# Mixing stage of a two-layer hybrid decoder: probability products in fp32, queries normed inside the scores, the key factor as a logarithm, Silu on ScalarE, and other constants for the order

## Chip, cores and metric

The kernel runs on one core of a Trainium2 chip. The metric is the device time of one execution in microseconds (us); the time of the kernel before is the median of its runs. The engines are PE (TensorE; PEld is its weight load), DVE (VectorE), ACT (ScalarE), POOL (GpSimd) and SP, which here issues all DMAs.

## What is computed

Two layers over 256 rows of 1024 numbers, all in fp32. Each layer is a SwiGLU half step, a mixing step with two groups of heads side by side, and a second SwiGLU half step. Cut to what the change touches:

```python
for l in range(2):
    x = x + 0.5 * swiglu(rmsnorm(x), ...)           # D_FF = 2816
    proj = rmsnorm(x) @ w_in[l]                      # q, k/v of three branches, gates, hq, hf, hi, hg
    # attention: 8 query heads of 64 in 2 groups; three branches of keys
    q = norm_rope(q); k_cmp, k_sel, k_win = norm_rope(...)   # RMS norm per head, then rotation
    o = g0 * softmax(q @ compressed_k) @ compressed_v + g1 * softmax(q @ k_sel) @ v_sel + g2 * softmax(q @ k_win) @ v_win
    # recurrence: 4 heads of 128, chunks of 64 rows
    q = silu(hq); f = lb + (1 - lb) * sigmoid(hf); k = 1 - f; v = hi
    b = cumsum(log f)
    a[t, s] = sum_k q[t, k] * exp(b[t, k] - b[s, k]) * k[s, k]    # s <= t, else 0
    o = rmsnorm(a @ v + carried state) * silu(hg)
    x = x + concat(attention, recurrence) @ w_out[l]
    x = x + 0.5 * swiglu(rmsnorm(x), ...)
```

## The kernel before

Rows are in two halves of 128 (`h` = 0, 1). All matrix products with weights run as three fp32r products, hi times hi, hi times lo and lo times hi: each number is split into an fp32r part `hi` (a copy on ACT) and a rest `lo` (a subtraction on DVE, at times on POOL). Weights arrive by DMA in units of 512 KB, and each unit is split the same way while the unit before it is used, so the stream itself costs one ACT copy (line 334) and one DVE subtraction (line 347) of 128x1024 for each unit.

The program is written out by a planner at build time (`Sched.run`). Every piece of work is a generator that hands in one operation at a time with a planned cost and the engines that may take it. The planner always issues the operation with the earliest planned start plus a penalty; the penalties stand in `PEN`, `STEP`, `PREP`, `FLOW`, `BIAS`, and `LAG` and `OUT_ORDER` shape the weight stream. So the constants set nothing but the order of instructions on each engine and which engine takes an operation that has a choice. Most operations are issued by helpers, so they share a line: 347 is a DVE `tensor_tensor`, 350 one on POOL, 334 an `activation`, 343 a DVE copy, 358 a DVE `tensor_scalar`, 360 one on POOL, 376 the power for inverse square roots on POOL, 382 transposes. They are told apart by their tiles.

In a mixing step the in-projection streams through in the order q, kv, kw, hf, hq, hi, hg. Meanwhile:

- `q_task` squares the projected queries (ACT), sums (DVE, line 896), takes the inverse root (POOL), multiplies (DVE, `buf<-acc,qst`) and frees the accumulator, then rotates. `kv_task`, `kw_task` and `values` split the values into `vh` and `vl`.
- `log_task` and `level_task` build the recurrence. `level_task` walks over seven block sizes; at each it makes left factors, exp of the running sum `S` times the key factor `kk` (`hx<-hx,kk`), and right factors, exp of `P` times the query (`hx<-hx,xn`), for small products on PE (line 1368) that are put into `ad` (line 1374).
- `head_task` (16 in each mixing step) makes scores on PE (lines 1174 and 1175), adds the mask and takes the row maximum in one DVE instruction for each of two branches (line 1178), scales the maxima by -1/8 (`mx<-mx`, line 358 or 360), takes Exp on ACT, and multiplies by gate over sum.
- `turn_task` (12 in each mixing step) transposes four heads' probabilities, copies them to `pth` (ACT), subtracts to get `ptl` (DVE); `attend_task` then issues for each of two halves three fp32r products of 256 columns with `vh` and `vl` (lines 1144 to 1146). `cmp_task` handles the compressed branch; its product (line 1158) is in plain fp32.
- `hq_task` and `hg_task` take Sigmoid on ACT and multiply by the projection on DVE (`xn<-hx,acc` and `G<-G,acc`).

Then the out-projection runs: the attention part needs `att`, the recurrence part needs `ho` of `out_task`.

Of the kernel before, what the change touches and what calls it, by code (L numbers as in the profile page):

```python
# [23 lines left out]
SCALE = DH ** -0.5  # L24
# [25 lines left out]
FIRST = (-0.3, -0.4, 0.5, 1.3, 0.1, 0.6, 0.9, 0.2)  # L50
LAG = 4
NBUF = 14
OUT_ORDER = ((0, 0), (0, 1), (1, 0), (1, 1))
# [3 lines left out]
PEN = {"norm_turn": 0.1, "next_gain": 2.25, "gates_task": 0.15, "compress_task": -0.05, "level_task": 0.25,  # L57
       "boot": -1.0, "first_gain": -0.3, "first_norm": -0.25, "pad": 3.35, "hi_task": -3.8, "load_stream": 3.25,
       "done": 0.25, "kv_task": 0.65, "turn": 2.65, "load_w1": 3.15, "mix_prepare": -0.2, "c_turn": -3.3,
       "f_task": 0.25, "q_turn": 0.05, "kw_task": -6.1, "q_task": 0.6, "hg_task": 0.75, "hq_task": 0.45,  # L60
       "last_product": -0.15, "k_turn": 0.15, "products": 0.05, "turn_task": -0.1, "attend_task": -0.05,
       "out_task": 0.05, "k_task": 0.4, "cmp_task": -0.1, "first_turn": -0.65, "head_task": -0.1, "log_task": 0.15}
STEP = {'h': -0.16, 'g': 0.03, 'r': 0.0}
PREP = (-0.2, 0.25, 0.55, 0.75)
FLOW = (0.25, 0.15, 0.15)
BIAS = {'POOL': 0.1, 'ACT': -0.05}
# [56 lines left out]
class Sched:  # L123
# [85 lines left out]
    def emit(self, t, eng, start, end, fn):  # L209
        fn()  # L210

    def run(self):
        while self.tasks:
# [28 lines left out]
            self.emit(t, eng, end - cost, end, fn)  # L242
# [42 lines left out]
def rel(x, *objs):  # L285
    return ("rel", x, objs)
# [18 lines left out]
class Trunk(Sched):  # L305
# [251 lines left out]
    def start(self):  # L557
# [14 lines left out]
        self.padded = [per.tile([128, 4, 320], F32R, name=n) for n in ("vh", "vl")]  # L572
# [10 lines left out]
    def pad(self):  # L583

        nc = self.nc
        vh, vl, gv, vcb = self.padded
        for t in [gv, vcb] + self.pcs:
            yield self.G(0.25, lambda: nc.gpsimd.memset(t, 0.0))
        z = vcb[:, 0:1, 0, :64].to_broadcast([128, 4, 64])
        for v in (vh, vl):  # L590
            for o in (0, 128, 256):
                yield self.G(0.97, lambda: nc.gpsimd.tensor_copy(v[:, :, o:o + 64], z))
        yield put("padded")
# [267 lines left out]
    def mix(self, l):  # L861
# [24 lines left out]
        def q_task(h, ps):  # L886
            yield wait(("open", p))
            yield wait(("prepared", l))
            bufs = yield acq("buf", 3)
            (pair,) = yield acq("pth")  # L890
            sq, xr, t2 = [x.rearrange("p (n d) -> p n d", d=64) for x in bufs]
            qd = [x.rearrange("p (n a d) -> p n a d", n=4, a=2) for x in pair]
            src = ps.rearrange("p (n d) -> p n d", d=64)
            st = M["qst", h]
            yield A(sq, src, AF.Square)
            yield V(512, lambda: nc.vector.tensor_reduce(st[:, 0], sq, AX.X, OP.add))
            yield from self.rope_norm(st, (H, DH))
            x_ = yield tt(xr, src, st[:, 0, :, None].to_broadcast([128, H, 64]), OP.mult)
            yield rel(f"acc{h}", ps)
            cg = self.cg[:, h, 0:1].to_broadcast([128, H, 64])  # L900
            a_ = [(yield tt(sq, xr, cg, OP.mult, pool=True))]
            for o, i in swap:
                a_.append((yield tt(t2[:, :, o], xr[:, :, i], self.sg[:, h, 0:1, o].to_broadcast([128, H, 32]), OP.mult,
                                    pool=True, after=[x_])))
            for b, d in enumerate(qd):
                c = slice(4 * b, 4 * b + 4)
                hi = d[:, :, 0]
                yield tt(sq[:, c], sq[:, c], t2[:, c], OP.add, pool=True, after=a_)
                yield self.copy(hi, sq[:, c])
                yield tt(d[:, :, 1], sq[:, c], hi.bitcast(F32), OP.subtract, pool=True)  # L910
                yield put(key("qd", h, b))
                sub(q_turn(h, b, pair, d), deps=self.keys[key("qd", h, b)])
            yield rel("buf", *bufs)
# [17 lines left out]
        def values(h, br, src):  # L931

            c = lambda v: v[:, 2 * br + h, 64:].rearrange("p (g d) -> p g d", g=2)[:, :, :64]
            yield from self.split(c(M["vh"]), c(M["vl"]), src)
# [169 lines left out]
        def attend_task(h, g):  # L1104
            for x in (("k", h), ("k", 0), ("q", h, g), ("g", h)):
                yield wait(key(*x))
# [23 lines left out]
            vh, vl, vcb = M["vh"], M["vl"], M["vcb"]  # L1130
# [4 lines left out]
            for i, (so, vi) in enumerate(tiles):  # L1135
                yield wait(key("pt", h, g, i))
                yield wait(key("v", vi % 2, vi // 2))
                th, tl = M["pt", h, g, i]

                def pv(e):  # L1140
                    o = 64 + 128 * g - 64 * e
                    c = slice(256 * e, 256 * e + 256)
                    f = nc.tensor.matmul
                    f(po[:, :256], vh[:, vi, o:o + 128], th[:, c], start=(i == 0 and e == 0), stop=False)
                    f(po[:, :256], vl[:, vi, o:o + 128], th[:, c], start=False, stop=False)
                    f(po[:, :256], vh[:, vi, o:o + 128], tl[:, c], start=False, stop=False)  # L1146

                for e in range(2):
                    yield P(0.36, lambda: pv(e))
                yield rel("pth", (th, tl))  # L1150
# [15 lines left out]
        def head_task(h, g, r, part, pr, mx):  # L1166

            qs, kh, kl, gt = M["qs", h], M["kh"], M["kl"], M["gt", h]
            mxr, smr = mx[:, 0, r], mx[:, 1, r]
            a, b, segs = part  # L1170
# [6 lines left out]
            for br, o, n, mask in segs:  # L1177
                yield V(n, lambda: nc.vector.tensor_tensor_reduce(pr[r][:, o:o + n], ps[:, o:o + n], mask, 1.0, -BIG, OP.add, OP.max,  # L1178
                                                                  mxr[:, br:br + 1]))
            yield rel("short", ps)  # L1180
            yield ts(mxr, mxr, -SCALE, pool=True)
            for br, o, n, mask in segs:
                x = pr[r][:, o:o + n]
                yield A(x, x, AF.Exp, bias=mxr[:, br:br + 1], scale=SCALE, accum_out=smr[:, br:br + 1])
# [9 lines left out]
        def turn_task(h, g, i, so, pr):  # L1194
            (pt,) = yield acq("short")
            yield self.transposes([(pt[:, 128 * k:128 * k + 128], pr[r][:, so:so + 128]) for k, r in enumerate((0, 2, 1, 3))])
            ((th, tl),) = yield acq("pth")
            yield from self.split(th, tl, pt)
            M["pt", h, g, i] = th, tl
# [3 lines left out]
        def cmp_task(h, g):  # L1203
# [19 lines left out]
            yield V(64, lambda: nc.vector.tensor_reduce(m, x, AX.X, OP.max))  # L1223
            yield tt(x, x, m[:, :, None].to_broadcast([128, R, 16]), OP.subtract, pool=True)
            yield A(x, x, AF.Exp, scale=SCALE)
# [35 lines left out]
        def log_task(h):  # L1261
# [12 lines left out]
            d_ = yield G(0.46, lambda: nc.gpsimd.memset(s_, 0.0))  # L1274
# [3 lines left out]
        def hq_task(c, ps):  # L1278
            yield wait(("open", p))
            (e,) = yield acq("hx")  # L1280
            yield A(e, ps, AF.Sigmoid)
            v = lambda x: x.rearrange("p (k h t) -> p k h t", k=2, h=2)
            yield tt(M["QQ"][:, :, 2 * c:2 * c + 2].rearrange("p h k t -> p k h t"), v(e), v(ps), OP.mult)
            yield rel(f"acc{c}", ps)
            yield put(key("hq", c))
            yield rel("hx", e)
# [7 lines left out]
        def hg_task(h, ps):  # L1294
            yield wait(("open", p))
            x = M["G2", h]
            yield A(x, ps, AF.Sigmoid)
            yield tt(x, x, ps, OP.mult)
# [8 lines left out]
        def level_task(h):  # L1307
# [9 lines left out]
            for i, hh in enumerate(LEVELS[1:] + [64]):  # L1317
# [11 lines left out]
                else:  # L1329
                    a_ = yield A(xl, sl, AF.Exp, after=prev + got)  # L1330
                    c_ = yield tt(xl, xl, kl, OP.mult, pool=True)
# [12 lines left out]
            yield tt(xc, xc, kk if h == 0 else q, OP.mult)  # L1344
# [115 lines left out]
        def opened(pool, p):  # L1460
# [3 lines left out]
            self.slots["hx"] = [(T([128, 512], f"hx{i}"), []) for i in range(4)]  # L1464
            self.slots["pth"] = [((T([128, 512], f"pth{i}", F32R), T([128, 512], f"ptl{i}", F32R)), []) for i in range(2)]
# [21 lines left out]
            M["vh"], M["vl"], M["gv"], M["vcb"] = self.padded  # L1487
# [64 lines left out]
```

## Time and profile before

| | |
|---|---|
| median of 3 runs (lowest to highest) | 1134.69 us (1132.74 to 1187.89) |
| profiled execution, its own time | 1132.6 us |
| its span, first to last instruction | 1130.8 us |
| busy: PE, DVE, ACT, POOL | 1090.8, 699.6, 577.1, 96.6 us |
| mean granted clock of PE | 0.972 of 2.4 GHz |

A group of instructions in the profile is one line, engine, operation and pair of tiles: `out<-in`, partitions x elements, count, then busy time in all, mean ns of one, and the idle time of the engine just before them. Tiles go by the names of the program (`short`, `acc` and `po` are PSUM; `kk`, `P`, `S`, `xn`, `mx`, `buf` are SBUF). Seen by stages, the two mixing steps lie at 205 to 394 us and 762 to 950 us; the rest are SwiGLU steps.

### The profile page before, as it was taken

The page shows a single profiled execution, that of the slowest core. Times are in us where ns is not written, and L with a number is a line of the kernel's source. Part 1 is how long each engine was busy: PE and PEld are TensorE (multiplying, and loading weights), DVE is VectorE, ACT ScalarE, POOL GpSimd, SP SyncE. Part 2 cuts the span into 40 slices and gives each one's busy share as a digit, 9 for nine tenths or more (in the row PEclk, how much of TensorE's full clock was granted, in tenths as well). Part 3 has the DMA queues.
Part 4 walks back from the last instruction along what each step waited for, and adds up shares of the span by engine and source line. Part 5 has one row for each costly group of instructions (what it writes and reads, how often), then busy time and mean ns, then how long its engine had stood idle before and what let it go on. Part 6 is the DMA issues. An engine that isn't in the chain of part 4 may idle for free.

```text
span 1130.8 us, 18755 instructions
## 1 busy us (share of the span) xinstructions
PE 1090.8 (96%) x7420; PEld 975.9 (86%) x7420; DVE 699.6 (62%) x1242; ACT 577.1 (51%) x911; POOL 96.6 (9%) x124
## 2 busy tenths in 40 slices
PE   6999999999889999999999999999997899999998
PEld 4999988898668799998889999888975788999986
DVE  5665544689985755554465555448898857555543
ACT  6544444467664554443454444435866645444432
POOL 3100000041121100000010000001403201000000
PEclk9999999999879999999999999999998699999999
DMA  7666666565501476666666666556544125666553
GB/s 223 209 197 172 189 185 188 161 174 168 169 20 38 149 207 185 186 185 187 188 179 195 187 179 187 185 168 187 165 137 131 38 75 168 196 180 186 185 160 120
DMA packets 154168, 186.16 MB, mean 165 GB/s; under 512 B 7568, under 2 KB 117984, under 8 KB 154080
## 3 DMA queue, kind: packets, MB, share of 16 engines
q1 hardware_dynamic: 154080, 184.96, 55.1%
q8 instruction: 58, 0.95, 0.3%
q14 instruction: 30, 0.25, 0.1%
HBM read 183.89 MB, written 1.05 MB: 164 GB/s over the span
## 4 chain that ended last, share of the span: by engine, by line
PE 85%; DVE 9%; DMA 2%; issue 2%; ACT 1%; POOL 1%; SPq 0%; DVEq 0%; ACTq 0%; POOLq 0%
PE acc L515 15%; PE acc L516 15%; PE acc L517 15%; PE acc L485 11%; PE acc L487 11%; PE acc L486 11%; PE short L382 2%; DVE lo L347 2%; DVE buf L1178 1%; PE short L1368 1%; DVE xn L690 1%; DMA lg<-in_hgrn_lb_logits_dram 1%; DVE hx L347 1%; PE po L1146 1%; DVE buf L358 1%
## 5 line engine op out<-in xcount | busy, mean ns | idle before, releaser
L347 DVE TENSOR_TENSOR lo<-raw,hi 128x1024 fp32r<-128x1024 f32 (+2 forms) x329 | 394.9, 1202 | 287.2 <-ACT hi L334 286.0
L334 ACT ACTIVATE hi<-raw 128x1024 fp32r<-128x1024 f32 (+2 forms) x337 | 351.6, 1045 | 317.4 <-PE acc L487 108.0
L515 PE MATMUL acc<-xh,hi 128*128 128x256 f32 x1408 | 399.2, 284 | 0.0
L517 PE MATMUL acc<-xh,lo 128*128 128x256 f32 x1408 | 398.4, 283 | 0.0
L516 PE MATMUL acc<-xl,hi 128*128 128x256 f32 x1408 | 398.4, 283 | 0.0
L515 PEld LDWEIGHTS acc<-xh,hi 128*128 128x128 f32 x1408 | 270.2, 192 | 0.2
L516 PEld LDWEIGHTS acc<-xl,hi 128*128 128x128 f32 x1408 | 270.3, 192 | 0.1
L517 PEld LDWEIGHTS acc<-xh,lo 128*128 128x128 f32 x1408 | 270.2, 192 | 0.0
L485 PE MATMUL acc<-hi,th 128*128 128x512 f32 x352 | 139.7, 397 | 0.0
L486 PE MATMUL acc<-lo,th 128*128 128x512 f32 x352 | 139.2, 395 | 0.0
L487 PE MATMUL acc<-hi,tl 128*128 128x512 f32 x352 | 139.2, 395 | 0.0
L485 PE MATMUL acc<-hi,xh 128*128 128x512 f32 (+1 forms) x240 | 95.8, 399 | 0.0
L487 PE MATMUL acc<-hi,xl 128*128 128x512 f32 (+1 forms) x240 | 91.7, 382 | 0.0
L486 PE MATMUL acc<-lo,xh 128*128 128x512 f32 (+1 forms) x240 | 91.2, 380 | 0.0
L487 PEld LDWEIGHTS acc<-hi,tl 128*128 128x128 f32 x352 | 66.1, 188 | 16.1
L486 PEld LDWEIGHTS acc<-lo,th 128*128 128x128 f32 x352 | 66.2, 188 | 15.5
L485 PEld LDWEIGHTS acc<-hi,th 128*128 128x128 f32 x352 | 66.2, 188 | 15.5
L334 ACT ACTIVATE sg<-acc 128x512 f32<-128x512 f32 (+1 forms) x46 | 26.2, 570 | 72.0 <-PE acc L517 68.8
L376 POOL TENSOR_TENSOR rs<-rs,half 128x1 f32<-128x1 f32 x12 | 7.0, 587 | 572.6 <-DVE rs L683 572.6
L487 PEld LDWEIGHTS acc<-hi,xl 128*128 128x128 f32 x240 | 45.4, 189 | 9.1 <-DVE xl L347 0.4
L485 PEld LDWEIGHTS acc<-hi,xh 128*128 128x128 f32 x240 | 45.5, 190 | 7.8
L486 PEld LDWEIGHTS acc<-lo,xh 128*128 128x128 f32 x240 | 45.5, 190 | 6.9
(230 smaller groups left out, 1100.1 us busy)
## 6 DMA issues: line engine op xcount, KB each, us to landing
raw<-in_ffn_w_down_dram SPq DMA_DIRECT2D x88, 512.0 KB, 4.2
raw<-in_ffn_w_gate_dram SPq DMA_DIRECT2D x80, 512.0 KB, 3.8
raw<-in_ffn_w_up_dram SPq DMA_DIRECT2D x80, 512.0 KB, 3.9
raw<-in_w_in_dram SPq DMA_DIRECT2D x48, 512.0 KB, 3.8
raw<-in_w_out_dram SPq DMA_DIRECT2D x16, 512.0 KB, 3.7
buf<-in_cmp_w_dram SPq DMA_DIRECT2D x16, 256.0 KB, 7.3
raw<-in_ffn_w_gate_dram SPq DMA_DIRECT2D x13, 256.0 KB, 2.8
raw<-in_ffn_w_up_dram SPq DMA_DIRECT2D x13, 256.0 KB, 3.1
```

The source lines that it names most:

```text
L334: return ("ACT", c, lambda: self.nc.scalar.activation(out, in_, func, **k), TABLES.get(func), False)
L347: alts = [("DVE", 0.065 + 0.00104 * n, lambda: self.nc.vector.tensor_tensor(out, a, b, op), None, not in_psum(a) and not in_psum(b))]
L358: lambda: self.nc.vector.tensor_scalar(out, a, s1, s2, **k), None, not in_psum(a))]
L382: self.nc.tensor.transpose(o, i, self.ident[:i.shape[0], :i.shape[0]])
L485: f(ps[:, :k.n], ah, hi[:, t, :k.n], start=st, stop=False)
L486: f(ps[:, :k.n], ah, lo[:, t, :k.n], start=False, stop=False)
L487: f(ps[:, :k.n], al, hi[:, t, :k.n], start=False, stop=sp)
L515: f(ps[:, c], hi[:, t, j], xh, start=u.first and c == t == 0, stop=False)
L516: f(ps[:, c], hi[:, t, j], xl, start=False, stop=False)
L517: f(ps[:, c], lo[:, t, j], xh, start=False, stop=u.last and c == 1 and t == 3)
L690: toks.append((yield self.V(576, lambda: nc.vector.scalar_tensor_tensor(self.XN[h][:, c], self.X[h][:, c], rs[:, 0:1], self.gains[0][:, c] ...
L1146: f(po[:, :256], vh[:, vi, o:o + 128], tl[:, c], start=False, stop=False)
```

## The change

Six edits of the mixing step and a new set of planner constants.

1. The transposed probabilities and the values are no longer split: `turn_task` makes one copy `th` (on ACT or DVE), `values` one copy `vh`, and each half is one fp32 product in place of three fp32r ones.
2. Queries are rotated straight out of PSUM without the norm. The norm factor, times -1/8, is a number per row and head (`nq`); the instruction of line 1178 multiplies by it and takes the minimum, so the scaling of the maxima is gone. `cmp_task` multiplies by it in an operation of its own. `attend_task` waits for it as well.
3. `log_task` puts log of the key factor into `S` where it wrote zeros, so that exp of `S` holds the key factor and six multiplications in each `level_task` go, and one more for `h` = 0.
4. `hq_task` and `hg_task` use Silu on ACT in place of Sigmoid and a product.
5. `pad` clears one tile of values with memsets where it cleared two with copies.
6. All the planner's constants are new, and the recurrence part of the out-projection takes its two column halves in the other order.

```diff
-LAG = 4
+LAG = 5
-OUT_ORDER = ((0, 0), (0, 1), (1, 0), (1, 1))
+OUT_ORDER = ((0, 0), (0, 1), (1, 1), (1, 0))
...
-       "done": 0.25, "kv_task": 0.65, "turn": 2.65, "load_w1": 3.15, "mix_prepare": -0.2, "c_turn": -3.3,
...
+       0.38, "kv_task": 0.73, "turn": 0.9, "load_w1": 2.81, "mix_prepare": 0.27, "c_turn": -3.2, "f_task": 0.07,
...
-BIAS = {'POOL': 0.1, 'ACT': -0.05}
+BIAS = {'POOL': 0.07, 'ACT': -0.49}
...
         def q_task(h, ps):
-            yield A(sq, src, AF.Square)
-            yield V(512, lambda: nc.vector.tensor_reduce(st[:, 0], sq, AX.X, OP.add))
-            yield from self.rope_norm(st, (H, DH))
-            x_ = yield tt(xr, src, st[:, 0, :, None].to_broadcast([128, H, 64]), OP.mult)
+            x_ = yield A(xr, src, AF.Square)
+            sub(q_norm(h, bufs[1], st), deps=[x_])
+            cg = self.cg[:, h, 0:1].to_broadcast([128, H, 64])
+            a_ = [(yield tt(sq, src, cg, OP.mult))]
+            for o, i in swap:
+                a_.append((yield tt(t2[:, :, o], src[:, :, i], self.sg[:, h, 0:1, o].to_broadcast([128, H, 32]), OP.mult)))
+            yield ("deps", a_)
             yield rel(f"acc{h}", ps)
...
+        def q_norm(h, buf, st):
+
+            yield V(512, lambda: nc.vector.tensor_reduce(st[:, 0], buf.rearrange("p (n d) -> p n d", d=64), AX.X, OP.add))
+            yield rel("buf", buf)
+            yield from self.rope_norm(st, (H, DH))
+            yield ts(st[:, 0], st[:, 0], -SCALE)
+            yield put(key("nq", h))
...
         def values(h, br, src):
-            yield from self.split(c(M["vh"]), c(M["vl"]), src)
+            yield self.copy(M["vh"][:, 2 * br + h, 64:].rearrange("p (g d) -> p g d", g=2)[:, :, :64], src)
...
         def attend_task(h, g):
-            for x in (("k", h), ("k", 0), ("q", h, g), ("g", h)):
+            for x in (("k", h), ("k", 0), ("q", h, g), ("g", h), ("nq", h)):
...
-                    f(po[:, :256], vh[:, vi, o:o + 128], th[:, c], start=(i == 0 and e == 0), stop=False)
-                    f(po[:, :256], vl[:, vi, o:o + 128], th[:, c], start=False, stop=False)
-                    f(po[:, :256], vh[:, vi, o:o + 128], tl[:, c], start=False, stop=False)
+                    nc.tensor.matmul(po[:, :256], vh[:, vi, o:o + 128], th[:, c], start=(i == 0 and e == 0), stop=False)
...
         def head_task(h, g, r, part, pr, mx):
-                yield V(n, lambda: nc.vector.tensor_tensor_reduce(pr[r][:, o:o + n], ps[:, o:o + n], mask, 1.0, -BIG, OP.add, OP.max,
+                yield V(n, lambda: nc.vector.tensor_tensor_reduce(pr[r][:, o:o + n], ps[:, o:o + n], mask, nq, BIG, OP.add, OP.min,
                                                                   mxr[:, br:br + 1]))
             yield rel("short", ps)
-            yield ts(mxr, mxr, -SCALE, pool=True)
...
         def turn_task(h, g, i, so, pr):
-            ((th, tl),) = yield acq("pth")
-            yield from self.split(th, tl, pt)
+            (th,) = yield acq("pf")
+            yield self.copy(th, pt)
...
         def cmp_task(h, g):
-            yield V(64, lambda: nc.vector.tensor_reduce(m, x, AX.X, OP.max))
-            yield tt(x, x, m[:, :, None].to_broadcast([128, R, 16]), OP.subtract, pool=True)
+            yield tt(x, x, M["qst", h][:, 0, R * g:R * g + R, None].to_broadcast([128, R, 16]), OP.mult)
+            yield V(64, lambda: nc.vector.tensor_reduce(m, x, AX.X, OP.min))
+            yield tt(x, x, m[:, :, None].to_broadcast([128, R, 16]), OP.subtract)
...
         def log_task(h):
-            d_ = yield G(0.46, lambda: nc.gpsimd.memset(s_, 0.0))
+            d_ = yield ts(s_, kk, tiny, op0=OP.max, after=[b_, c_], pool=True)
+            d_ = yield A(s_, s_, AF.Ln)
...
         def hq_task(c, ps):
-            yield A(e, ps, AF.Sigmoid)
-            v = lambda x: x.rearrange("p (k h t) -> p k h t", k=2, h=2)
-            yield tt(M["QQ"][:, :, 2 * c:2 * c + 2].rearrange("p h k t -> p k h t"), v(e), v(ps), OP.mult)
+            yield A(M["QQ"][:, :, 2 * c:2 * c + 2].rearrange("p h k t -> p k h t"),
+                    ps.rearrange("p (k h t) -> p k h t", k=2, h=2), AF.Silu)
...
         def hg_task(h, ps):
-            yield A(x, ps, AF.Sigmoid)
-            yield tt(x, x, ps, OP.mult)
+            yield A(x, ps, AF.Silu)
...
         def level_task(h):
                     a_ = yield A(xl, sl, AF.Exp, after=prev + got)
-                    c_ = yield tt(xl, xl, kl, OP.mult, pool=True)
+                    c_ = a_
...
-            yield tt(xc, xc, kk if h == 0 else q, OP.mult)
+            if h:
+                yield tt(xc, xc, q, OP.mult)
```

## Rows read from the trace of the kernel before

**Rows 1.** The page, part 1: busy time, share of the span, instructions.

```profile
PE 1090.8 (96%) x7420; PEld 975.9 (86%) x7420; DVE 699.6 (62%) x1242; ACT 577.1 (51%) x911; POOL 96.6 (9%) x124
```

**Rows 2.** Windows: stretch, length, busy of PE, PEld, DVE, ACT, POOL; clock, DMA.

```profile
205.00:262.00 57.00, 57.00 (x372) 51.86 (x371) 46.94 (x91) 39.88 (x67) 15.56 (x10) 1.00 0.56 160
262.00:296.00 34.00, 33.77 (x287) 25.93 (x287) 31.68 (x74) 21.26 (x38) 3.38 (x9) 1.00 0.51 155
296.00:315.00 19.00, 15.63 (x161) 12.43 (x158) 16.59 (x92) 13.50 (x49) 5.61 (x7) 0.73 0.57 166
315.00:363.00 48.00, 41.35 (x250) 33.99 (x249) 36.06 (x130) 29.10 (x77) 10.10 (x16) 0.82 0.11 34
...
851.00:871.00 20.00, 16.22 (x154) 12.16 (x150) 16.92 (x95) 13.93 (x51) 5.42 (x7) 0.74 0.54 156
871.00:918.00 47.00, 40.84 (x249) 33.89 (x249) 36.14 (x128) 28.71 (x76) 10.08 (x16) 0.82 0.11 35
```

**Rows 3.** Chain that ended last, first mixing step: start, length, engine, tile, line.

```profile
287.69 0.66 DVE hx L347 x2
...
300.57 0.42 DVE mx L358
...
311.65 0.69 DVE ptl L347
...
321.07 0.08 DVE mx L358
...
322.93 1.04 PE short L1215 x4
```

**Rows 4.** Groups by line and form on DVE, whole run: what goes.

```profile
L347 DVE TENSOR_TENSOR ptl<-short,pth 128x512 fp32r<-128x512 f32 x24 | 16.1, 688 | 9.9 <-ACT pth L334 9.9
L347 DVE TENSOR_TENSOR hx<-hx,kk 128x256 f32<-128x256 f32 x18 | 8.3, 458 | 0.0
L358 DVE TENSOR_SCALAR mx<-mx 128x2 f32<-128x2 f32 x24 | 5.0, 215 | 0.0
L347 DVE TENSOR_TENSOR xn<-hx,acc 128x512 f32<-128x512 f32 x4 | 2.7, 684 | 0.1
L347 DVE TENSOR_TENSOR G<-G,acc 128x512 f32<-128x512 f32 x4 | 2.7, 682 | 0.0
L347 DVE TENSOR_TENSOR buf<-acc,qst 128x512 f32<-128x512 f32 x4 | 2.7, 682 | 0.0
L347 DVE TENSOR_TENSOR vl<-acc,vh 128x128 fp32r<-128x128 f32 x8 | 2.3, 290 | 6.6 <-ACT vh L334 6.6
L347 DVE TENSOR_TENSOR S<-S,kk 128x512 f32<-128x512 f32 x2 | 1.4, 692 | 0.1
```

**Rows 5.** The same view of DVE: rows nearest to what comes.

```profile
L358 DVE TENSOR_SCALAR kk<-kk 128x512 f32<-128x512 f32 x4 | 1.7, 424 | 0.1
L347 DVE TENSOR_TENSOR pc<-pc,short 128x64 f32<-128x64 f32 x8 | 1.7, 213 | 0.0
L347 DVE TENSOR_TENSOR sg<-acc,sg 128x256 f32<-128x256 f32 x6 | 2.6, 425 | 4.1 <-ACT sg L334 3.1 <-DMA raw<-in_ffn_w_up_dram 1.0
L730 DVE SCALAR_TENSOR_TENSOR sg<-acc,rs,sg 128x256 f32<-128x256 f32 x2 | 0.9, 472 | 0.0
```

**Rows 6.** The chain again: products with values, fp32r (1145) and fp32 (1158).

```profile
348.35 0.12 PE po L1145
...
348.94 0.44 PE po L1158 x4
```

**Rows 7.** ACT timeline, first mixing step: a table load and what follows it.

```profile
244.34 1.28 ACT L241 ACT_TABLE_LOAD   x1
245.63 0.34 ACT L334 ACTIVATE gt<-gt 128x24 f32<-128x24 f32 x2
```

**Rows 8.** Groups by line and form on ACT, whole run.

```profile
L334 ACT ACT_TABLE_LOAD x11 | 14.1, 1283 | 0.9 <-PEq L1538 0.7
L334 ACT ACTIVATE P<-P 128x512 f32<-128x512 f32 x6 | 3.8, 628 | 3.3 <-DVE P L347 3.3
```

## Prediction before the run

> **What bounds the kernel now.** I read the busy shares first. PE is busy 96% of the span and DVE 62% [rows 1], so the kernel looks bound by PE and the other engines look idle enough. That is an average, and the change touches only the two mixing steps, so the second view is the windows by stage [rows 2]. In the first mixing step PE is full up to 296 us (57.00 of 57, 33.77 of 34): nothing that another engine saves there can shorten it directly. From 296 to 363 us PE has 19 - 15.63 + 48 - 41.35 = 10.0 us without work, and its granted clock is 0.73 and 0.82, that is, parts of it at 1.2 in place of 2.4 GHz; 0.27 x 19 + 0.18 x 48 = 13.8 us is what the low clock takes at most. The second mixing step repeats this between 851 and 918 us (10.0 and 13.7 us). So some 24 us for each step is all that any edit here can win; DVE meanwhile is busy 31.68 of 34 and 16.59 of 19 us.
>
> The third view says who is waited for: the chain of waits in that stretch [rows 3]. Between 287.69 and 322.93 us nearly all of its pieces are DVE's, back to back, of which four stand in the rows; the exceptions are one transfer of keys near 299 us and, from 307.4 to 311.6 us, transposes, small products and one ACT copy. So for 35 us PE waits for DVE's queue and not for any single result. After 322.93 us the chain is mostly PE, in part at the low clock, with single DVE pieces between. What the change is worth is therefore read from DVE's queue in the first stretch and from PE in the second.
>
> **What leaves DVE.** By groups [rows 4], for both steps: the rests of the transposed probabilities 16.1 us, the products with the key factor 8.3 and 1.4, the scaling of the maxima 5.0, the Sigmoid products 2.7 and 2.7, the query norm 2.7, the rests of the values 2.3: 41.2 us, 20.6 for each step.
>
> **What comes to DVE** [rows 5]. Four operations of 128x512 that limit the key factor, at 0.424 us: 1.7 us (POOL may take some). Eight products in the compressed branch at 0.213 us: 1.7 us. Four small scalings of the query norm, no dearer than that: 0.9 us. The 64 score instructions get a factor for each row instead of a constant; no row shows that instruction with one. The nearest pair are products out of PSUM of 256 elements with and without such a factor, 0.472 and 0.425 us: 0.047 us each, 3.0 us in all. From below it is 0, as the instruction multiplies by a constant already, and a gain has no reason since it gets longer in nothing but the operand; from above it is the whole of the scaling that it replaces, 0.215 us for two, 6.9 us in all. I take 3.0, the price of the nearest row. Together 7.3 us; DVE's net relief is 33.9 us, 17.0 for each step.
>
> **What comes to PE.** Each of 48 halves has one fp32 product of 256 columns for three fp32r ones. In the chain an fp32r product takes 0.12 us (0.35 for three), and the four records of two fp32 products of 128 columns take 0.44 us [rows 6]; 256 columns in fp32 are thus 0.44 us. The difference is 0.09 us, 2.1 us for each step at full clock, 4.3 at half. Bounds: 0 if the one product saves two waits between products, 4.3 if all of them fall in low clock. I take 2.1 and put it on the path, because these products lie in the stretch that PE leads.
>
> **What comes to ACT.** Two more logarithms of 128x512 for each step, 0.628 us each [rows 8]: 1.3 us. Silu costs what Sigmoid does, but hf keeps Sigmoid, so the order of hf, hq, hg may need up to two more table loads for each step, at 1.28 us [rows 7, 8]: 0 to 2.6 us. I take them at nothing, since ACT is busy 13.50 of 19 and 29.10 of 48 us [rows 2] and waits for DVE there; without that cover they would cost all of their 3.9 us. In the rows a table load is followed by the next activation 0.01 us after its end [rows 7]. The Trainium skill, ScalarE: Activation LUTs, section What ACT_TABLE_LOAD costs, adds a drain of about 1.38 us to each load, 2.66 us for a switch; by that, two more loads would be 5.3 us for each step in place of 2.6, and the trace does not agree, as nothing of that length follows a load.
>
> **The sum at an unchanged order, one step.** In the stretch that DVE leads: the scaling of the maxima is on the chain nine times, from the piece at 300.57 to that at 321.07 us, 1.5 us together [rows 3]. The rest at 311.65 us is on it with 0.69 us; the one at 309 us is not. Five key products at 0.33 us (two such pieces in 0.66 us [rows 3]) give 1.7. What DVE is spared before, where it is 93% busy (262 to 296 us [rows 2]), carries in: two Sigmoid products of hq, 1.4 us, four key products, 1.3, less two limits, 0.85: 1.8 us. The query norm and the rests of the values, 2.5 us, lie before 262 us, where DVE has pauses (46.94 of 57 us); I count half, 1.2. The score instructions take back 28 x 0.047 = 1.3 us. Sum: 5.6 us. In the stretch that PE leads: three rests of probabilities are on the chain with 1.9 us together; against them stand 2.1 us of longer products and some 0.4 us of the compressed branch: -0.6. The Sigmoid products of hg and the other rests lie beside PE and bring nothing. That makes 5.0 us for a step and 10 us in all.
>
> The rest costs nothing: `pad` works on POOL during the first SwiGLU step; queries leave their accumulator earlier, but PE is full there; the other order of column halves may move one norm by 1 to 2 us either way. The added wait of `attend_task` is for a number that is ready some 65 us earlier; behind it on its engines nothing is queued, as a planner places the instructions.
>
> **The order.** 17.0 us leave DVE in each step, and the sum above uses 7.1 of it (5.0, and 2.1 that PE takes back). The other 10 are slack in places where PE is full. New constants can turn slack into an earlier start of the heads under the weight stream, or fail to. I take a quarter, 2.5 us for a step, 5 in all; the ends are 0 and all of it. The gain is 15 us. The profiled execution took 1132.6 us, 1.8 more than its span and 2.1 less than the median of the runs. So 1132.6 - 15 = 1117.6, and on the scale of the median 1119.7: I say 1120 us.
>
> **Rivals.** (1) The order turns everything into time: (17.0 - 2.1) x 2 = 29.8 us, 1105 us. For it: the reserve of 24 us a step is large enough, and heads without pauses would keep PE at 2.4 GHz. Against it: in the heads ACT is close behind DVE (71% of 296 to 315 us [rows 2]) and nothing is taken from it.
>
> (2) ACT becomes the bound. It gets 3.9 us a step, logarithms and two table loads, just where exponentials are waited for; then 10 - 7.8 = 2.2 us of gain stay, 1132.5 us. Against it: ACT is busy only 51% [rows 1]. The Trainium skill, same page, section Table sets: the hidden batching unit, says to group activations by table set, which speaks against a second function beside Sigmoid; the trace shows the switch at 1.28 us.
>
> (3) The other side: PE's fp32 products set the time, and what DVE is spared stays hidden. They lie between the transposes and the out-projection, where PE is on the chain; the price is 4.3 us, 1137 on the profile's scale and 1139 on the median's, up to 1143 if all run at half clock. It decides if DVE's relief brings less than 2.1 us a step. Against it: 35 us of DVE pieces on the chain.
>
> (4) The change doesn't do what it says: copies of probabilities may go to ACT or DVE, and if the planner puts all 24 on DVE, at the 0.69 us of what went, 16.5 us of the relief are gone; half of the gain stays, 1127 us. Against it: the constants favour ACT by 0.49 us.
>
> **Chances.** Forecast (1112 to 1129) 0.50; rival 1 (1098 to 1112) 0.22; rival 2 (1129 to 1136) 0.12; rival 3 (1136 to 1145) 0.11; rival 4 0.05. No more than about 2% can be told from no change in this kernel, that is 1112.0 to 1157.4 us. Faster by over 2% is rival 1: 0.22. Slower by over 2% needs rival 3 and a lost overlap besides: 0.02. Within: 0.76. The range reaches to 1103 and 1137: it leaves out the better half of rival 1 and most of rival 3, less than 0.2, and takes in 0 to 6.9 us for the score instructions.
>
> **What will show it.** The chain between the first heads and the last products should be shorter by 5 to 10 us a step, with fewer DVE pieces; DVE's busy time should be about 666 us, PE's idle time in that stretch below 10 us. The products with values should show about 0.44 us for a half. If ACT pieces, table loads among them, stand where DVE pieces stood, it is rival 2; if the stretch is as long as before and PE is full, rival 3; if the clock stays whole from heads to out-projection, rival 1. I am wrong if the new order moves the heads to where PE has no other work, or if score instructions grow by more than 0.1 us.

## Result, and the profile after

The kernel after takes 1094.48 us (median of 4 runs, 1093.81 to 1095.44), against 1133.72 us for the kernel before beside it (median of 4). One of those four runs, at 1187.89 us, was in a slow state and is left out of the ratio, which is 0.9666, 95% interval 0.9637 to 0.9695. That is 38 to 39 us where 15 were predicted, and it is outside the predicted range of 1103 to 1137 us. The profiled execution took 1094.78 us and its span is 1093.0 us, 37.8 less than before.

Part 1 of the page of the kernel after (it answers to [rows 1]):

```profile
PE 1068.4 (98%) x7372; PEld 960.0 (88%) x7372; DVE 666.3 (61%) x1151; ACT 579.6 (53%) x945; POOL 57.9 (5%) x88
```

PE is busy 22.4 us less and idle 15.4 us less (24.6 in place of 40.0). These two are the whole 37.8 us. Less busy time does not mean less work here: with all edits in the order of before PE is busy 1091.6 us, and with none of them in a new order 1070.3 (e1 and e5 below). What fell is time at the low clock; the mean granted clock is 0.995 in place of 0.972. The windows of the kernel after, columns as in [rows 2]:

```profile
262.00:296.00 34.00, 31.98 (x271) 25.45 (x269) 30.94 (x128) 28.83 (x87) 2.99 (x4) 0.95 0.57 156
296.00:315.00 19.00, 18.39 (x136) 14.86 (x136) 16.34 (x77) 17.50 (x55) 2.35 (x6) 0.91 0.20 60
315.00:363.00 48.00, 45.96 (x323) 37.11 (x321) 31.60 (x53) 29.31 (x54) 7.68 (x8) 1.00 0.35 107
...
871.00:918.00 47.00, 44.66 (x244) 37.02 (x244) 31.08 (x42) 24.65 (x37) 5.87 (x5) 1.00 0.39 118
```

From 262 to 363 us PE idles 4.7 us where it idled 10.3, and the clock is 0.95, 0.91 and 1.00 where it was 1.00, 0.73 and 0.82 [rows 2]. Counted as in the prediction, the low clock takes at most 0.05 x 34 + 0.09 x 19 = 3.4 us in place of 13.8. An estimate from these rows is thus 5.6 us won in pauses and up to 10.4 by the clock; it is rough, as the same windows hold other work in each kernel. The work has changed places: from 262 to 296 us DVE has 128 instructions in place of 74 and ACT 87 in place of 38. The heads now begin there, among the units of the weight stream: the first score product starts at 270.33 us (298.97 before). The chain of waits of the kernel after in the same stretch:

```profile
273.77 0.27 DVE buf L1176
274.10 0.39 PE short L1172
...
275.70 0.43 PE acc L482
...
276.98 1.47 PE short L1364 x32
...
299.96 0.43 PE acc L482
...
302.85 0.38 DVE buf L1176
...
313.89 1.73 PE po L1143 x8
...
324.35 0.44 PE po L1155 x4
```

L1176 is the score instruction, L1172 a score product, L482 a product of the weight stream, L1364 one of the recurrence, L1143 one with values. In the chain before [rows 3], 35 us of nearly nothing but DVE pieces stood with no stream product between them; here stream products stand among the heads from 275.70 to 281 and from 298.68 to 301 us, and again from 310 us. Between these the pieces are still ACT's and DVE's, for 16 and 9 us. The residual sums, whose last one ends the mixing step in each kernel, come at 363.93 in place of 383.33 us in the first mixing step, and 16.5 of these 19.4 us are won after the last residual sum ahead of it (208.90 and 211.80 us). In the second mixing step the same count gives 18.1 us.

Two rows of DVE in the groups of after, and the same instruction before, name what got dearer:

```profile
L1176 DVE CUSTOM_DVE_ANT_0 buf<-short,con,qst 128x256 f32<-128x256 f32 x32 | 14.5, 477 | 0.0
...
L1176 DVE CUSTOM_DVE_ANT_0 buf<-short,con,qst 128x128 f32<-128x128 f32 x32 | 9.2, 342 | 0.1
```

```profile
L1178 DVE CUSTOM_DVE_ANT_0 buf<-short,con 128x256 f32<-128x256 f32 x32 | 13.2, 413 | 1.0 <-PE short L1175 1.0
L1178 DVE CUSTOM_DVE_ANT_0 buf<-short,con 128x128 f32<-128x128 f32 x32 | 8.2, 280 | 1.0 <-PE short L1175 1.0
```

The factor for each row, with a minimum in place of the maximum, costs 0.063 us at either size. On ACT, the groups after with table loads and the copies of probabilities (all 24 on ACT):

```profile
L331 ACT ACTIVATE pf<-short 128x512 f32<-128x512 f32 x24 | 13.4, 593 | 9.0 <-PE short L379 4.9 <-PE po L1143 4.1
L331 ACT ACT_TABLE_LOAD x9 | 11.5, 1283 | 2.0 <-PE acc L484 1.1 <-PEq L1535 0.7
...
L238 ACT ACT_TABLE_LOAD x7 | 9.0, 1283 | 0.1
```

There are 16 loads; before had 20 (the 11 of [rows 8] and 9 from line 241).

### The profile page after: what moved, and what is told of

Read it like the earlier page. It is cut to its first block, busy times and chain, and to the rows that moved or that the text cites. A ratio compares the mean times of both kernels' runs of the same rounds, so it can differ in the third digit from the quotient of the medians.

```text
span 1093.0 us, 18540 instructions
## 1 busy us (share of the span) xinstructions
PE 1068.4 (98%) x7372; PEld 960.0 (88%) x7372; DVE 666.3 (61%) x1151; ACT 579.6 (53%) x945; POOL 57.9 (5%) x88
## 3 DMA queue, kind: packets, MB, share of 16 engines
HBM read 183.89 MB, written 1.05 MB: 169 GB/s over the span
## 4 chain that ended last, share of the span: by engine, by line
PE 88%; DVE 7%; ACT 2%; DMA 1%; issue 1%; SPq 0%; POOL 0%; DVEq 0%; POOLq 0%
PE acc L513 15%; PE acc L512 15%; PE acc L514 15%; PE acc L482 12%; PE acc L483 11%; PE acc L484 11%; PE short L379 2%; PE po L1143 2%; DVE buf L1176 1%; PE short L1364 1%; DVE xn L685 1%; DMA gain<-in_ffn_norm_dram 1%; DVE lo L344 1%; DVE buf L344 1%; DVE P L344 0%
## 5 line engine op out<-in xcount | busy, mean ns | idle before, releaser
L344 DVE TENSOR_TENSOR lo<-raw,hi 128x1024 fp32r<-128x1024 f32 (+2 forms) x334 | 400.8, 1203 | 293.5 <-ACT hi L331 288.1
L331 ACT ACTIVATE hi<-raw 128x1024 fp32r<-128x1024 f32 (+1 forms) x336 | 351.0, 1046 | 308.1 <-PE acc L484 106.4
L482 PE MATMUL acc<-hi,th 128*128 128x512 f32 x352 | 139.7, 397 | 0.0
L482 PE MATMUL acc<-hi,xh 128*128 128x512 f32 (+1 forms) x240 | 94.9, 395 | 0.0
L482 PEld LDWEIGHTS acc<-hi,th 128*128 128x128 f32 x352 | 66.2, 188 | 15.7
L483 PEld LDWEIGHTS acc<-lo,th 128*128 128x128 f32 x352 | 66.2, 188 | 15.4
L482 PEld LDWEIGHTS acc<-hi,xh 128*128 128x128 f32 x240 | 46.1, 192 | 7.7 <-issue 0.4
L344 DVE TENSOR_TENSOR sg<-acc,sg 128x512 f32<-128x512 f32 (+1 forms) x46 | 30.2, 656 | 27.2 <-PE acc L514 24.1
```

The lines of the kernel that those rows point to most:

```text
L331: return ("ACT", c, lambda: self.nc.scalar.activation(out, in_, func, **k), TABLES.get(func), False)
L344: alts = [("DVE", 0.065 + 0.00104 * n, lambda: self.nc.vector.tensor_tensor(out, a, b, op), None, not in_psum(a) and not in_psum(b))]
L482: f(ps[:, :k.n], ah, hi[:, t, :k.n], start=st, stop=False)
L483: f(ps[:, :k.n], ah, lo[:, t, :k.n], start=False, stop=False)
```

## Experiments

In the expectations, theory A says that the gain is DVE's relief, made into time by a new order; B, that the relief alone brings it; C, that the constants alone bring it. F to L are defined where they come. "Held order" means that the planner of before works with its own costs and places every instruction as before, and the code that it then issues is the changed one; an operation that goes leaves no work, and one that comes is issued beside its neighbour (`swap_fn` keeps an operation's place and planned cost and replaces what it issues; `also` issues one more instruction behind it).

### Edits or constants

**e1_edits_old_order**: all six edits, order of before held.

```diff
-            yield tt(xr, src, st[:, 0, :, None].to_broadcast([128, H, 64]), OP.mult)
+            yield swap_fn(tt(xr, src, st[:, 0, :, None].to_broadcast([128, H, 64]), OP.mult), turn)
...
-            yield ts(mxr, mxr, -SCALE, pool=True)
+            yield swap_fn(ts(mxr, mxr, -SCALE, pool=True), None)
```

> All edits, but every instruction stands where the planner put its forerunner in the kernel before: removed instructions are planned and then left out, new ones stand beside the one they belong to, and all constants are the old ones. This measures the sum of the prediction at an unchanged order, 10 us of gain. Theory A (the edits are worth little until the order changes): 1120 to 1128 us, and PE's granted clock in the heads of the mixing steps stays near 0.75 and 0.82. Theory B (DVE's relief alone does it, the order is secondary): 1100 to 1108 us with the clock above 0.95 there. Theory C (the constants alone did it): about 1134 us.

**e2_edits_old_constants**: the code of after with all constants of before, placed by the planner.

> All edits, with the old planner constants (penalties, lag, column order of the out-projection), the planner free to place everything anew. Theory A: between the run at the old order and the changed kernel, 1108 to 1120 us, as the planner moves the heads only as far as the old penalties let it. Theory B: 1095 to 1100 us. Theory C: no better than the run at the old order, 1122 to 1135 us.

**e3_old_code_new_constants**: the code of before with all constants of after.

> The kernel before with the new planner constants and the new column order alone, none of the edits. Theory A (constants fitted to the new work need its relief of DVE): 1120 to 1140 us. Theory B: 1130 to 1140 us. Theory C (the weight stream spread among the heads is what counts, and any code can have it): 1098 to 1112 us.

**e4_new_order_old_work**: the order of after, with DVE given back the work that the edits had taken, as maxima and scalings in place that change no number (the query norm's is not put back).

```diff
-            yield self.copy(th, pt)
+            yield also(self.copy(th, pt), lambda: nc.vector.tensor_tensor(th, pt, th, OP.max))
```

> The changed kernel in its own order, with DVE loaded again: beside each place where an instruction was removed from DVE (rests of probabilities and values, scaling of maxima, key products, Silu products) stands one of the same size that takes the maximum of a tile with itself, in place. The query norm's is not put back. DVE gets about 38 us back, PE and ACT keep the new work. Theory A (the relief is what lets the new order pay): 1115 to 1130 us. Theory C (the order holds whatever DVE does): 1095 to 1105 us. If DVE's instructions were simply added to the path one by one, 1132 us.

| kernel | median us | ratio to before, 95% interval |
|---|---|---|
| e1_edits_old_order | 1127.95 | 0.9979 (0.9966 to 0.9991) |
| e2_edits_old_constants | 1133.21 | 1.0015 (1.0002 to 1.0028) |
| e3_old_code_new_constants | 1113.18 | 0.9842 (0.9819 to 0.9865) |
| e4_new_order_old_work | 1119.64 | 0.9903 (0.9883 to 0.9924) |

The edits alone bring 2 us or nothing; the constants alone bring 18 us, on code in which DVE has nearly all its old work (691.0 us). In the order of after, the relief is worth the difference between 0.9903 and 0.9666, some 27 us (25 by the medians), for 33.5 us of DVE work (699.8 against 666.3). Each operation put back stands between its neighbour and what uses the result, as the old one did, so the load on DVE and the longer wait are not told apart. Of the ranges, e1 and e4 lie in A's; e2 lies in C's, 13 us above A's; e3 lies between C's and A's, 1.2 us above C's. So B falls, and A and C each hold a part: 11 us (e4) to 18 us (e3) of the 38 need no relief, and the rest is relief that the new order turns into time. Windows of e1 show what the old order does with it:

```profile
296.00:315.00 19.00, 15.69 (x151) 12.23 (x150) 14.42 (x76) 12.46 (x48) 4.49 (x5) 0.64 0.64 184
315.00:363.00 48.00, 43.61 (x246) 35.92 (x246) 30.46 (x123) 30.40 (x80) 8.02 (x11) 0.86 0.12 34
```

DVE is busy 5.6 us less than before from 315 to 363 us, and PE still idles 3.3 and 4.4 us, at a granted clock of 0.64 and 0.86. Its chain:

```profile
297.14 0.59 PE short L1397 x16
...
300.31 0.44 DVE kl L363
...
309.00 1.11 PE short L398 x4
310.11 1.72 PE short L1084 x24
311.83 1.05 PE short L398 x4
312.88 1.94 PE short L1084 x39
...
317.45 0.48 DVE buf L1200
...
325.39 1.03 PE short L1238 x4
```

Up to 298 us the chain is PE now, with the stream: the DVE pieces that stood there [rows 3] had run beside a full PE, and what DVE is spared there is hidden. The first scores still wait for the last part of the keys, whose piece `kl` begins at 300.31 us (298.94 before). From 309 to 317 us PE leads, at a granted clock of 0.53 from 305 to 315 us: four transposes (L398) take 1.11 and 1.05 us where they take 0.44 at 343.60 us. Then DVE's pieces lead once more, to the compressed scores at 325.39 us (L1238; L1215 at 322.93 in the chain before [rows 3]). From the first score product to these it is 25.1 us in e1 and 24.0 before, in the second mixing step 25.1 and 24.7. So in these executions the relief shortened nothing up to there; the first step is shorter only behind it, with its last residual sum at 380.67 in place of 383.33 us.

### Which constant

**e5_old_code_flow** and **e6_edits_flow** (on the code of e2) change one line:

```diff
-FLOW = (0.25, 0.15, 0.15)
+FLOW = (0.19, 0.28, 0.45)
```

> The code of before, with one constant of after alone: FLOW, the stream's three numbers, 0.19, 0.28, 0.45 for 0.25, 0.15, 0.15. In the order of PE's instructions this puts 42 products of the weight stream between the first and the last score products of a mixing step, where before has 2. Theory F (what the constants are worth is that heads stand among the stream's units, so that PE has full work and its clock while DVE serves both): about as fast as the old code with all new constants, 1112 to 1118 us, and the granted clock from 296 to 315 us above 0.9. Rival G (the gain is spread over many constants): 1126 to 1133 us.

> All six edits of the code with the constants of before, except FLOW from after. 28 stream products stand between the first and the last scores of a mixing step (none with the old FLOW, 36 in the kernel after). Theory F: most of the gain comes with this one constant, 1096 to 1108 us. Rival G: 1120 to 1133 us, close to the 1133 of the same code with the old FLOW.

**e7_after_lag4** is the kernel after with `LAG = 4`, **e8_after_old_pen** the kernel after with the dictionary `PEN` of before.

> The kernel after, with LAG 4 in place of 5 and nothing else; FLOW stays new. In its order the heads of a mixing step no longer stand among the stream: 4 stream products lie between the first and the last scores, in place of 36. Theory F: the gain goes with them, 1118 to 1133 us, and the clock in the heads falls again to 0.6 to 0.8. Rival G (the other constants and FLOW carry the gain wherever the heads stand): 1094 to 1102 us.

> The kernel after, with the 34 penalties of PEN from before and the other constants new. The heads stay among the stream (38 stream products between the first and the last scores of the first mixing step, 40 in the second). Theory F: little is lost, 1094 to 1104 us. Rival G (the penalties make a good part of the gain): 1106 to 1125 us.

| kernel | median us | ratio to before, 95% interval |
|---|---|---|
| e5_old_code_flow | 1111.08 | 0.9827 (0.9806 to 0.9848) |
| e6_edits_flow | 1117.34 | 0.9883 (0.9862 to 0.9905) |
| e7_after_lag4 | 1116.49 | 0.9871 (0.9846 to 0.9897) |
| e8_after_old_pen | 1098.61 | 0.9718 (0.9696 to 0.9739) |

Three of four went F's way: three numbers of the stream give the old code all that the whole set of constants gives it; taking the heads out of the stream again costs 23 us; the 34 penalties are worth 6 us (0.9718 against 0.9666; 4 by the medians). Only e8 lies in F's range; e5 is 0.9 and e7 1.5 us below it, all three are 7 us or more from G's, and in e7 the granted clock fell less than F gave (0.91 and 0.86, not 0.6 to 0.8). LAG 4 could also have starved the stream, but in e7 PE waits for no transfer of weights. F missed with e6 by 9 us: with the edits, FLOW alone makes the kernel no faster than without them. The windows of e5 and e7:

```profile
262.00:296.00 34.00, 33.88 (x245) 27.96 (x244) 32.13 (x146) 28.92 (x83) 3.30 (x12) 1.00 0.68 187
296.00:315.00 19.00, 18.72 (x157) 16.09 (x157) 18.72 (x75) 16.71 (x47) 3.46 (x7) 1.00 0.34 112
315.00:363.00 48.00, 38.76 (x356) 31.62 (x355) 40.54 (x86) 24.94 (x48) 7.39 (x10) 0.89 0.25 78
```

```profile
296.00:315.00 19.00, 13.37 (x123) 9.85 (x123) 15.05 (x76) 16.61 (x62) 2.15 (x4) 0.91 0.48 137
315.00:363.00 48.00, 46.07 (x254) 39.00 (x255) 28.92 (x98) 32.78 (x82) 2.92 (x6) 0.86 0.18 55
```

In e5, with heads among the stream, PE is full at a whole clock to 315 us with no relief at all; DVE is nearly as full (32.13 of 34, 18.72 of 19 us), and PE's 9.2 idle us come after 315 us. In e7 the pauses of the heads are back, 5.6 us from 296 to 315 us; after them the clock is 0.86, where it is 1.00 in the kernel after.

### What the relief is worth, and what the clock

**e9_edits_flow_order**: the edits as in e1, in the held order of e5.

> All six edits, put into the exact instruction order that the code of before gets with the new FLOW alone (1111 us without the edits); the planner sees the old costs, so nothing is placed anew. Theory F: DVE is the bound in that order (84% busy and PE idle for 9.2 us between 315 and 363 us), so its relief is worth there what it is worth in the order of after, 15 to 25 us: 1087 to 1097 us. Rival H (relief turns into time only where a planner places the instructions anew): 2 to 5 us as in the old order held, 1106 to 1109 us.

**e10_new_order_pv_back** and **e11_new_order_others_back** split e4: its added operations for the probabilities and values alone, and all its others alone.

> The order and work of after, and on DVE one operation put back for each split that the first edit removed: 24 of 128x512 out of PSUM behind the copies of the probabilities and 8 of 128x128 behind those of the values, as maxima in place that change no number; some 18 us of DVE work. Theory F: all work that DVE gets counts where heads stand in the stream, so this is 18/38 of the 25 us that all of the old work cost: 1104 to 1109 us. Rival I (these operations lie at the transposes, late in the mixing step, where PE leads; the head work is what counts): 1094 to 1100 us.

> The same for the other edits: 32 small scalings of the maxima, the key products of the levels and the Silu products put back on DVE, as operations in place that change no number; some 20 us of DVE work; the probabilities and values stay unsplit. Theory F: 1105 to 1111 us. Rival I: nearly all of the 25 us, 1113 to 1119 us.

**e12_old_order_scores_twice**: e1 with each score product issued twice.

```diff
-                nc.tensor.matmul(ps[:, :b - a], qs[:, R * g + r], kh[:, g, a:b], start=True, stop=False)
-                nc.tensor.matmul(ps[:, :b - a], qs[:, R * g + r], kl[:, g, a:b], start=False, stop=True)
+                for _ in range(2):
+                    nc.tensor.matmul(ps[:, :b - a], qs[:, R * g + r], kh[:, g, a:b], start=True, stop=False)
+                    nc.tensor.matmul(ps[:, :b - a], qs[:, R * g + r], kl[:, g, a:b], start=False, stop=True)
```

> All six edits in the order of before held (1128 us), and each score product on PE issued twice into the same place, some 24 us more of PE work for the whole kernel; the numbers stay. Theory F in its part on the clock (PE runs at 1.2 GHz in the heads because it pauses there): the added work fills the pauses, the granted clock from 296 to 315 us rises from 0.64 to above 0.9, and the time stays within 1122 to 1135 us. Rival J (the clock falls for another reason and PE's pauses are DVE's time): the clock stays near 0.64 and the time grows by the added products at half clock, 1140 us or more.

| kernel | median us | ratio to before, 95% interval |
|---|---|---|
| e9_edits_flow_order | 1118.21 | 0.9883 (0.9868 to 0.9898) |
| e10_new_order_pv_back | 1106.24 | 0.9778 (0.9763 to 0.9793) |
| e11_new_order_others_back | 1106.46 | 0.9781 (0.9764 to 0.9798) |
| e12_old_order_scores_twice | 1130.00 | 0.9985 (0.9974 to 0.9997) |

In the order of after both parts of the relief count: e10 and e11 lose 0.0112 and 0.0115 of 1131 us, 12.7 and 13.0 us, for 15.5 and 20.1 us of DVE work, and together as much as e4. Rival I falls: the rests of the probabilities cost no less than the head work.

e12 has 64 products more and takes as long as e1 within the intervals. Its windows:

```profile
296.00:315.00 19.00, 14.76 (x150) 12.11 (x152) 14.47 (x75) 12.70 (x47) 4.50 (x5) 0.84 0.67 194
315.00:363.00 48.00, 43.48 (x284) 36.16 (x277) 31.34 (x124) 30.48 (x81) 8.04 (x11) 0.96 0.12 34
```

The granted clock is 0.84 and 0.96 in place of 0.64 and 0.86, and PE is busy no longer than in e1 from 296 to 363 us, 58.2 against 59.3 us, with the added products in it. J falls; of F, the clock above 0.9 was not reached before 315 us, the time was. So the clock of this stretch follows the work that PE is given: with more of it in the same order, it rose. The Trainium skill, TensorE: Matmul & The Clock Gate, section What's actually happening, says that PE's recent activity releases its clock; this run agrees. PE's idle time did not shrink (4.2 in place of 3.3 us from 296 to 315 us), and the higher clock only paid for the added products; no run shows what a whole clock alone would bring.

e9 went the wrong way, 6 us slower than e5. Its waits on PE (us in all, times, longest) and its ACT timeline name one reason:

```profile
PE short L398 <- ACT buf L350: 2.7, 1, 2.7
```

```profile
266.05 0.63 ACT L1300 ACTIVATE S<-S 128x512 f32<-128x512 f32 x1 [2.23 <-DVE S L1299]
266.70 1.28 ACT L1310 ACT_TABLE_LOAD   x1
```

The added logarithm (L1300) waits 2.23 us for its limit, which stands late in DVE's queue; behind it on ACT stands the work of the keys, and PE waits 2.7 us. Three runs ask whether that is all.

**e13_flow_order_no_log** is e9 without the logarithm's edit, **e14_flow_order_log_alone** e9 with that edit only, **e15_old_order_no_log** e1 without it.

> The edits without the one on the logarithm, in the exact order that the code of before gets with the new FLOW (1111 us without edits, 1118 with all of them). Theory K (in that order the added Ln waits on ACT for its limit on DVE, 0.78 and 2.23 us, holds the stream's copies behind it and brings PE's low clock and a different meeting of queues; the relief itself pays): 1093 to 1103 us. Rival L (relief pays in no order that was not made for it): 1108 to 1120 us.

> The logarithm's edit alone in the same held order: two Ln and two limits for each mixing step, some 9.7 us of key products less on DVE. Theory K: slower than 1111 us for the waits of ACT, 1112 to 1120 us. Rival L: about 1111 us, 1107 to 1112.

> The edits without the logarithm's, in the exact order of before. There PE waited for nothing of ACT's Ln up to 300 us. Theory F (the relief of DVE is hidden behind PE in that order): 1126 to 1131 us, as with all edits (1128). Rival K carried over (the Ln spoils this order too): 1112 to 1122 us.

| kernel | median us | ratio to before, 95% interval |
|---|---|---|
| e13_flow_order_no_log | 1113.93 | 0.9844 (0.9819 to 0.9868) |
| e14_flow_order_log_alone | 1116.42 | 0.9871 (0.9842 to 0.9900) |
| e15_old_order_no_log | 1132.90 | 1.0020 (1.0001 to 1.0038) |

The logarithm seems to account for most of e9's loss: e9 and e13 differ by 0.0039, or 4 us, and e14 is 5 us slower than e5, in K's range and not in L's, though the intervals touch in both pairs. Without it the relief still brings nothing in that order, and e13 lies in L's range. So K is right on the logarithm and wrong on the relief. In the order of before the logarithm spoils nothing: e15 without it has none of the 2 us of e1, and lies 2 us above what F gave. Where the relief goes in e13 is seen in its windows, and in those of e5 for the same stretch:

```profile
315.00:335.00 20.00, 20.00 (x225) 16.33 (x223) 16.86 (x39) 15.90 (x31) 4.82 (x7) 1.00 0.10 29
335.00:345.00 10.00, 3.89 (x52) 3.25 (x51) 9.61 (x25) 4.39 (x11) 0.00 (x0) 0.62 0.59 187
```

```profile
315.00:335.00 20.00, 18.17 (x219) 15.39 (x217) 19.75 (x46) 15.59 (x31) 5.05 (x7) 1.00 0.14 46
335.00:345.00 10.00, 5.04 (x57) 3.91 (x58) 9.81 (x24) 3.96 (x8) 0.31 (x1) 0.62 0.56 176
```

Up to 335 us DVE is no longer full and PE has no gap; then PE idles 6.1 us in place of 5.0. The chain of e13 names what is late next in this execution:

```profile
328.82 0.40 ACT hx L350
...
329.23 1.28 ACT L1322
...
331.63 0.68 ACT L241
...
333.79 4.00 DMA raw<-in_w_out_dram
...
339.27 0.76 DVE hx L363 x2
```

Two table loads and the weights of the out-projection: a copy on ACT waits for them, and the exponentials of the recurrence stand behind it. In that order these transfers run late (DMA share 0.10 to 335 us, 0.59 after); in the kernel after it is 0.41 and 0.35 in the same two windows.

## Why the prediction was wrong

**What bounds the kernel** was read rightly: 24 us for each step as all that can be won held (16.5 and 18.1 us won). That PE waits for DVE's queue held only after 296 us, and even there a shorter queue alone brought nothing (e1).

**The sum at an unchanged order** failed first: 10 us predicted, 2 measured (e1). Its 1.8 and 1.2 us that "carry in" and its five key products counted DVE pieces up to 296 us at full price. They are on the chain [rows 3], but beside a PE that is full there [rows 2]; without them the chain is PE's, and the heads began no earlier. The terms behind them, the scalings and the rest at 311.65 us, did not show either: from the first score product to the compressed scores e1 takes 25.1 us for 24.0, with PE at half clock where DVE pieces went.

**The order** is the step that decided. I priced it as a share of DVE's slack, 2.5 us for a step, with ends from 0 to all of it. The sum has no term for the clock, though 13.8 of the 24 us were the clock's. But an order can bring time without any relief: e3 and e5 bring 18 and 19 us with the old DVE work, because the stream fills the pauses of the heads and keeps the clock. In the order of after, which with the old work brings 11 us (e4), the relief brings some 27 us. No sum over DVE's relief could have shown this; it could be suspected from [rows 2], where PE idles at a low clock right behind a stretch in which it is full. The other side of it, that relief in another order brings nothing, is e9 and e13, in an order taken from the code without it, and e2 and e6, where the planner placed the edited code by other constants.

**Rival 1** named the right end and the right sign, a clock nearly whole from the heads to the out-projection (0.91 and 1.00), but its 1105 us rested on the same cap, DVE's 29.8 us. The objection to it, that ACT is close behind DVE, did not hold: ACT is busy 17.50 of 19 us from 296 to 315 us, and PE is at 18.39.

**Terms that held.** DVE's busy time is 666.3 us, 666 predicted; partly by luck, since the planner also gave DVE five units of the stream that POOL had (POOL's `lo<-raw,hi` 5 in place of 10), and in the order of before it is 671.8, a relief of 27.8 us where 33.9 were predicted. The products with values: 1.73 us for four halves in the chain, 0.43 us each as against 0.44. Score instructions grew by 0.063 us each, 0.047 predicted, 4.0 us in place of 3.0 and far from the 0.1 named as dangerous.

**Rivals 2 to 4** did not come. 2: four table loads fewer, not more, and no drain behind one (a load at 263.07 us takes 1.28, the activation behind it starts at 264.37). 3: PE's busy time fell, and with the edits in the order of before it is 0.8 us above that of before (1091.6 against 1090.8). 4: all copies of the probabilities are on ACT.

What stays open: why the planner with the edits and the new FLOW alone (e6) comes out no better than the edits put into e5's order. PE's longest single wait in its first mixing step is 4.0 us, of the compressed scores for ACT; in the kernel after the same scores wait 0.2 us at most. No run took it apart.

## What to carry to other kernels

When the bound engine pauses in one stage and is full in the one before it, look first for work of the full stage that can be held back as filler; that is worth the pause and the low clock together, and can be had with no change to the work (here 19 us from three numbers). A relief of another engine is priced at the order that will run, not at the one in the trace: the edits brought 2 and -6 us in two held orders (e1, e9 against e5), and their relief of DVE 27 us in a third (after against e4). A piece on the chain that ran beside a full bound engine brought nothing when it went.

## What the runs showed of the hardware

Adding 64 products, 32 in each mixing step, where PE pauses cost no measurable time, while the clock granted there rose from 0.64 to 0.84 and from 0.86 to 0.96 in the first step. A factor from a tile in place of a constant in the score instruction costs 0.063 us for 128 as for 256 columns, so at these two sizes it is a fixed price. A load of an activation table takes 1.28 us, and the next activation starts 0.02 us after it.
